# A fused decoder layer on one core: c spread by TensorE transposes, squares on two engines, sums of squares mixed with warm-up passes

## The chip, the core and the metric

The kernel runs on one core of a Trainium2 chip. The time is device microseconds of one execution. Engines are named as the profile names them: PE is TensorE's matmul side, PEld its weight loads, DVE VectorE, ACT ScalarE, POOL GpSimd, SP SyncE, which issues nearly all transfers (DMA) here.

## What is computed

One layer of a hybrid decoder over 256 positions of width 1024, in float32. A vector `c` conditions it:

```python
mod = jax.nn.silu(c) @ w_ada + b_ada            # 6 x 1024: shift, scale, gate, twice
h = rms_norm(x, norm1_g) * (1 + scale1) + shift1
x = x + gate1 * hybrid_token_mixer(h, ...)      # h @ w_in, attention and a state-space part, @ w_out
h = rms_norm(x, norm2_g) * (1 + scale2) + shift2
x = x + gate2 * conv_ffn(h, ...)                # up, causal conv, SwiGLU, down
```

What matters here is the start: `silu(c)`, the products of it with the rows of `w_ada`, and the mean square of every position of `x`, whose inverse root scales `h` ahead of the first projection.

## The kernel before

`x` stands transposed: `xT` has 128 partitions, 8 blocks `kt` of the width, 256 positions. All weights stream from HBM through a ring of eight raw buffers of 128x1024. Most are split into a high part (`whi`, ScalarE, L189) and a low part (`wlo`, VectorE, L191), and a product is three matmuls (high with high, low with high, high with low). The rows of `w_ada` come through buffers of their own (`ada`, `adax`); VectorE multiplies each with `silu(c)` and sums along the row (`ada_dve`, L239), which gives one column of `mod`.

`advance()` issues transfers on SyncE in a fixed list, and goes on as buffers come free. The first are `c`, two halves of `xT`, the first `ada`, part of `vec`, the second `ada`, then weights. `c` is read as one row into all 128 partitions of `cb` (L215), and ScalarE takes its silu in place (L233); `sc` is that tile.

From L221 to the end of the first stage every engine keeps the written order (`manual_schedule`); behind it a scheduler places the work of the stage that follows, on every engine. The front on TensorE:

- 22 passes of a matrix of ones with itself into bank 2 (L228), whose result nobody reads. They are the warm-up.
- `rms_sum` (L264): for each of the eight squared blocks two matmuls with one column of ones (L267), which add up the sums of squares for the two halves of the positions in bank 7. ScalarE takes the root (L270), VectorE the two `ada` products of `modulate1` and the reciprocal (L272).
- `keep_warm(n, out)` (L294) gives `n` more such passes: one here (`P["w0"]`), then `rms_transpose` (L289), two transposes that spread the result over the partitions, then four (`P["w1"]`).
- The first stage proper: for `kt` 0 matmuls with `hhi`, `hlo` (L412), the first v matmuls (`v0_mm`, L398), then the other blocks.

The squares `sq8` come from VectorE for blocks 0 to 3 (L325) and from ScalarE for 4 to 7 (L323), which loads the table for the root ahead of them (the activation into `warm`, L235). For `kt` 0, `s1_h` on ScalarE splits the first half of a weight chunk, writes `hhi`, `h` and `rb`, and then splits the second half; the first four matmuls use the first half, the next four the second. `v0_evac` copies the v results out of PSUM, half of them on ScalarE (L403), ahead of the next weight split there.

Of the kernel before, what the change touches and what calls it, by code (L numbers as in the profile page):

```python
# [11 lines left out]
AF = mybir.ActivationFunctionType  # L12
# [29 lines left out]
V_DTB = 326  # L42
V_ALL = 327

P = {'n2l': 6, 'sqa': 0, 'xr0': 0, 'scp': 1, 'vq': 1, 'v1': 6, 'n2': 4, 'hpx': [1, 0, 1, 0, 0, 1], 'e0': 0, 'ev': [1, 0, 1, 0], 'ada_u': [3, 4, 5, 5, 6, 7, 10, 9, 9, 19, 20, 20, 22, 24, 24, 25, 33, 35, 36, 37, 39, 39, 41, 42], 'ada_e': [1, 1, 1, 1, 1, 1, 1, 1, 1, 1, 1, 1, 1, 1, 1, 0, 1, 1, 1, 0, 1, 1, 0, 1], 'ada_lead': 4, 'ada_s': 0, 'g2': 68, 'hip': [0, 0, 0, 0, 0, 0, 0, 0, 0, 0, 0, 0, 0, 0, 0, 0, 0, 0, 0, 0, 0, 0, 0, 0, 0, 0, 0, 0, 0, 0, 1, 0, 0, 0, 1, 0, 0, 0, 0, 1, 0, 0, 0, 0, 0, 0, 0, 0, 0, 0, 0, 0, 0, 0, 0, 0, 0, 0, 0, 0], 'conv': [0, 0, 1, 0, 2, 5, 5, 4, 8, 4, 7, 6], 'dt': [1, 2, 2, 4], 'cdb': [7, 7], 'xbt': [9, 12, 11, 12], 'Y0': 14, 'DL': 3, 'ab0': 11, 'ss': 9, 'so': 2, 'qk': [12, 14, 17, 20, 21, 23], 'A0': 21, 'so1': 2, 'so2': 3, 'pv0': 26, 'sm_e': [0, 0, 1, 0, 1, 2, 2, 2], 'dc_e': [2, 0, 2, 0, 2, 0, 2, 0, 2, 0, 2, 0, 2, 0, 2, 0], 'mm_e': [1, 1, 1, 1, 1, 1, 1, 1, 1, 1, 1, 1, 1, 1, 1, 1], 'gz_e': [0, 0, 0, 0, 0, 0, 0, 0], 'sq_e': [1, 1, 1, 1, 1, 1, 1, 1], 'final': 2, 'ab_q': 0, 'LA': 2, 'asu': 34, 'aru': 38, 'aod': 2, 'w0': 1, 'w1': 4, 'w2': 4, 's1la': -1, 'zi': 1, 'lop': [0, 0, 0, 0, 0, 0, 0, 0, 0, 0, 0, 0, 0, 0, 0, 0, 0, 0, 0, 0, 0, 0, 0, 0, 0, 0, 0, 0, 0, 0, 0, 0, 0, 0, 0, 0, 0, 0, 0, 0, 0, 0, 0, 0, 0, 0, 0, 0, 0, 0, 0, 0, 0, 0, 0, 0, 0, 0, 0, 0], 'subs': [2, 1, 1, 1, 1, 1, 1, 1, 1, 1, 1, 1, 1, 1, 1, 1], 's1a': [0, 1, 0, 1, 0, 0, 0, 0]}

@with_exitstack
def mixer_ffn(ctx: ExitStack, tc: tile.TileContext, xT_d, c_d, vec_d, alog_d, ada_d,
# [155 lines left out]
    def get(la=LA):  # L204
        prep(la)
        i = st["get"]
        st["get"] += 1
        return ready.pop(i)

    cb = T([128, 1024], "cb")  # L210
    vec = T([128, V_ALL], "vec")
    alog = T([128, SH], "alog")
    xT = T([128, KT, S], "xT")

    sp.dma_start(cb, bass.AP(tensor=c_d.tensor, offset=c_d.offset, ap=[[0, 128], [1, D]]))  # L215
# [8 lines left out]
    pool.memset(epsc, EPS)  # L224
    ones = T([128, 128], "ones")
    pool.memset(ones, 1.0)
    for j in range(22):
        pe.matmul(bank[2][:, 0:128], ones, ones, start=True, stop=True)  # L228
    ident = T([128, 128], "ident")
    make_identity(nc, ident)  # L230
    mod = T([128, 48], "mod")
    sc = cb
    act.activation(sc, cb, AF.Silu)  # L233
    warm = T([128, 1], "warm")
    act.activation(warm, epsc, AF.Sqrt)  # L235

# [24 lines left out]
    rb2 = T([128, S], "rb2")  # L261
    acc = T([128, S], "accs")

    def rms_sum(parts, n, pb, between=lambda: None):  # L264
        for i, p in enumerate(parts):
            for t in range(2):
                pe.matmul(pb[:, t:t + 1], p[:, t * 128:(t + 1) * 128], ones[:, 0:1], start=(i == t == 0),  # L267
                          stop=(i == len(parts) - 1), skip_group_check=True)
        r = rt()
        act.activation(r[:, 2:4], pb[:, 0:2], AF.Sqrt, bias=epsc, scale=1.0 / n)  # L270
        between()
        dve.reciprocal(r[:, 0:2], r[:, 2:4])  # L272
        return r
# [15 lines left out]
    def rms_transpose(r, pb):  # L289
        for t in range(2):  # L290
            i = pe.transpose(pb[:, 256 + t * 128:384 + t * 128], r[:, t:t + 1].to_broadcast([128, 128]), ident)
        return i

    def keep_warm(n, out):  # L294
        for _ in range(n):
            pe.matmul(out, ones, ones, start=True, stop=True)
# [10 lines left out]
        return s  # L307


    sq8 = T([128, KT, S], "sq8", tag="big_x")  # L310
    sc1 = T([128, 2 * KT], "sc1")
    tri = T([128, 384], "tri")
    pool.memset(tri, 1.0)
# [43 lines left out]
    def s1_acc(i):  # L357
# [6 lines left out]
    final = (list(range(8)) + [12, 14, 15, 13, 8, 9, 10, 11], list(range(6)) + [14, 15, 12, 13, 8, 9, 10, 11, 6, 7],  # L364
             list(range(8)) + [14, 15, 12, 13, 8, 9, 10, 11], list(range(4)) + [14, 15, 12, 13, 8, 9, 10, 11, 4, 5, 6, 7])[P['final']]
# [58 lines left out]
    for kt in range(KT):  # L424
        if kt == 0:
# [5 lines left out]
            w0 = get(0)  # L431
# [310 lines left out]
    Y0, DL = P["Y0"], P["DL"]  # L742
# [21 lines left out]
    A0 = P["A0"]  # L764
# [23 lines left out]
    for i in range(5):  # L788
# [6 lines left out]
        c = st["get"] - 1  # L795
# [252 lines left out]
```

## Time and profile before

| | |
|---|---|
| three runs | 437.31, 437.0, 436.76 us; median 437.0 |
| the profiled execution | 437.12 us, of which the span is 435.4 us |
| PE / PEld / DVE / ACT / POOL busy | 98% / 89% / 78% / 59% / 8% of the span |
| chain that ended last | PE 84%, DVE 7%, ACT 5% |
| mean granted TensorE clock | 0.996 |
| HBM read | 95.14 MB, 221 GB/s over the span |

The span goes from the first to the last instruction; the time of a run has about 1.7 us around it. A row of the timeline gives the start, the length from the first start to the last end, engine, line, operation, what is written and read, the shape, how many, and in brackets the idle time ahead of it and what ended it. A matmul's recorded length is longer than its distance to the next one, since matmuls are pipelined: what a stream costs is read from the distance of starts. A float32 matmul of ones stands as two records (44 for 22 calls), a transpose as one.

### The profile page before, as it was taken

Reading aid. Unit: us, or ns where it says so; the run is one execution under the profiler, and the core shown is the slowest. Engines: PE = TensorE matmul, PEld = TensorE weight load, DVE = VectorE, ACT = ScalarE, POOL = GpSimd, SP = SyncE. Lnnn points to the kernel's source line nnn. Section 1 sums busy time; section 2 is a strip of 40 time slices with the busy share of each in tenths; the row PEclk is TensorE's granted clock in tenths of the full one; section 3 lists DMA queues with packets and bytes.
Section 4 is the critical chain, followed back from the end, with each engine's and each line's share of the span. In section 5 each row is a group of like instructions: output and inputs, shape, how many; then the busy total and the mean of one; then the engine's idle time right before and its main releaser. Section 6 shows DMA issues by size and latency. Waiting matters only on the chain.

```text
span 435.4 us, 7753 instructions
## 1 busy us (share of the span) xinstructions
PE 428.0 (98%) x2952; PEld 387.7 (89%) x2952; DVE 338.7 (78%) x670; ACT 259.0 (59%) x513; POOL 34.6 (8%) x31
## 2 busy tenths in 40 slices
PE   8999999999999999999999899999999999999996
PEld 9799998768766668888999699999999999999996
DVE  2779968999788998668699489787877876776655
ACT  4365448826998965642258386567766655555540
POOL 2000000000000020201220000032233200000000
PEclk9899999999999999999999999999999999999999
DMA  7999964899277644057790527866776565454002
GB/s 283 400 415 408 394 200 172 306 325 336 74 279 276 219 164 176 17 201 250 294 390 11 230 109 240 296 239 202 278 255 233 204 219 184 169 193 147 2 2 96
DMA packets 29589, 96.71 MB, mean 222 GB/s; under 512 B 3552, under 2 KB 6000, under 8 KB 29552
## 3 DMA queue, kind: packets, MB, share of 16 engines
q1 hardware_dynamic: 29520, 96.20, 61.1%
q8 instruction: 23, 0.38, 0.4%
q14 instruction: 14, 0.11, 0.1%
q10 hardware_dynamic: 32, 0.02, 0.0%
HBM read 95.14 MB, written 1.06 MB: 221 GB/s over the span
## 4 chain that ended last, share of the span: by engine, by line
PE 84%; DVE 7%; ACT 5%; issue 1%; DMA 1%; POOL 1%; ACTq 0%; POOLq 0%
PE bank L338 15%; PE bank L339 15%; PE bank L340 15%; PE bank L847 6%; PE bank L798 4%; PE bank L819 4%; PE bank L821 4%; PE bank L823 3%; PE bank L822 3%; DVE adax L239 2%; PE bank L412 2%; PE bank L228 2%; ACT whi L189 2%; DVE wlo L191 2%; PE bank L919 1%
## 5 line engine op out<-in xcount | busy, mean ns | idle before, releaser
L191 DVE TENSOR_TENSOR wlo<-raw,whi 128x1024 fp32r<-128x1024 f32 (+2 forms) x107 | 132.8, 1242 | 17.8 <-ACT whi L189 17.7
L189 ACT ACTIVATE whi<-raw 128x1024 fp32r<-128x1024 f32 (+2 forms) x106 | 108.6, 1032 | 39.8 <-PE bank L340 23.7
L338 PE MATMUL bank<-h2hi,whi 128*128 128x256 f32 x336 | 95.4, 285 | 2.1 <-ACT h2hi L889 1.9
L339 PE MATMUL bank<-h2hi,wlo 128*128 128x256 f32 x336 | 94.5, 283 | 0.0
L340 PE MATMUL bank<-h2lo,whi 128*128 128x256 f32 x336 | 93.9, 284 | 0.0
L338 PEld LDWEIGHTS bank<-h2hi,whi 128*128 128x128 f32 x336 | 64.4, 192 | 3.7 <-ACT h2hi L889 3.2
L339 PEld LDWEIGHTS bank<-h2hi,wlo 128*128 128x128 f32 x336 | 64.4, 192 | 0.0
L340 PEld LDWEIGHTS bank<-h2lo,whi 128*128 128x128 f32 x336 | 63.8, 192 | 0.2 <-DVE h2lo L890 0.2
L905 DVE SCALAR_TENSOR_TENSOR fbuf<-bank,vec,fbuf 128x255 f32<-128x255 f32 x84 | 40.3, 481 | 29.4 <-ACT fbuf L903 28.1
L244 POOL TENSOR_TENSOR ada<-ada,cb 128x1024 f32<-128x1024 f32 x11 | 28.8, 2621 | 270.2 <-DMA ada<-in_ada_dram 270.2
L338 PE MATMUL bank<-fsp,whi 128*128 128x256 f32 x176 | 49.8, 284 | 0.0
L339 PE MATMUL bank<-fsp,wlo 128*128 128x256 f32 x176 | 49.7, 283 | 0.0
L340 PE MATMUL bank<-fsp,whi 128*128 128x256 f32 x176 | 49.6, 283 | 0.0
L903 ACT ACTIVATE fbuf<-bank,vec 128x256 f32<-128x256 f32 x42 | 23.4, 560 | 36.2 <-PE bank L340 36.2
L239 DVE SCALAR_TENSOR_TENSOR ada<-ada,cb 128x1024 f32<-128x1024 f32 x27 | 32.8, 1216 | 3.0 <-DMA ada<-in_ada_dram 3.0
L338 PEld LDWEIGHTS bank<-fsp,whi 128*128 128x128 f32 x176 | 33.8, 192 | 0.1
L339 PEld LDWEIGHTS bank<-fsp,wlo 128*128 128x128 f32 x176 | 33.8, 192 | 0.0
L340 PEld LDWEIGHTS bank<-fsp,whi 128*128 128x128 f32 x176 | 33.7, 192 | 0.0
L821 PE MATMUL bank<-whi,hhi 128*128 128x512 f32 x70 | 29.5, 422 | 0.0
L847 PE MATMUL bank<-y,raw 128*128 128x256 f32 x128 | 28.9, 380 | 0.0
L822 PE MATMUL bank<-wlo,hhi 128*128 128x512 f32 x70 | 28.6, 408 | 0.0
L823 PE MATMUL bank<-whi,hlo 128*128 128x512 f32 x70 | 28.3, 405 | 0.0
(214 smaller groups left out, 783.1 us busy)
## 6 DMA issues: line engine op xcount, KB each, us to landing
raw<-in_wup_dram SPq DMA_DIRECT2D x44, 512.0 KB, 4.1
ada<-in_ada_dram SPq DMA_DIRECT2D x38, 512.0 KB, 5.1
raw<-in_wdn_dram SPq DMA_DIRECT2D x22, 512.0 KB, 3.6
raw<-in_winq_dram SPq DMA_DIRECT2D x16, 512.0 KB, 4.8
raw<-in_wout_dram SPq DMA_DIRECT2D x16, 512.0 KB, 3.8
adax<-in_ada_dram SPq DMA_DIRECT2D x10, 512.0 KB, 9.6
raw<-in_win_dram SPq DMA_DIRECT2D x8, 456.0 KB, 9.7
raw<-in_win_dram SPq DMA_DIRECT2D x7, 512.0 KB, 9.8
```

The source lines that it names most:

```text
L189: act.activation(hi[:, c], t[:, c], AF.Copy)
L191: (pool if lo_on_pool(i) else dve).tensor_tensor(lo[:, c], t[:, c], hi[:, c].bitcast(F32), op=OP.subtract)
L239: dve.scalar_tensor_tensor(t, t, 1.0, sc, op0=OP.mult, op1=OP.mult, accum_out=mod[:, i:i + 1])
L244: pool.tensor_tensor(adas[i], adas[i], sc, op=OP.mult)
L338: pe.matmul(out, w[0], h[0], start=start, stop=False, skip_group_check=True)
L339: pe.matmul(out, w[1], h[0], start=False, stop=False, skip_group_check=True)
L340: pe.matmul(out, w[0], h[1], start=False, stop=stop, skip_group_check=True)
L821: pe.matmul(bs[t], hhi[:, kt, blk(t)], w[0][:, wc], start=(q4 == k2 == 0), stop=False)
L822: pe.matmul(bs[t], hhi[:, kt, blk(t)], w[1][:, wc], start=False, stop=False)
L823: pe.matmul(bs[t], hlo[:, kt, blk(t)], w[0][:, wc], start=False, stop=(kt == KT - 1))
L847: pe.matmul(sacc(d), w[:, blk(kt)], X["y32"][:, kt], start=(kt == d % 2 == 0), stop=(kt == 7), skip_group_check=True)
L905: dve.scalar_tensor_tensor(a[:, s:], src[:, :S - s], vec[:, w + 2 - s:w + 3 - s], a[:, s:], op0=OP.mult, op1=OP.add)
```

## The change

- `c` comes as a tile `ccol` of 128 partitions by 8 columns (the host lays it out so). Eight TensorE transposes, each of one column broadcast to 128 wide, write it to banks 0 and 1, so that every partition has all of c; ScalarE takes the silu of each bank into one half of `cb`.
- The first warm-up has 10 passes instead of 22; eight passes stand behind the c transposes.
- ScalarE squares blocks 4 and 5 ahead of the table load, VectorE 0, 1, 2, 3, 6 and 7.
- `rms_sum` gets `fill`: ahead of every pair of sum matmuls but the first, three passes. The blocks are summed in the order 0, 1, 2, 3, 4, 6, 5, 7.
- Five passes stand ahead of the root's transposes instead of one, eight behind them instead of four. `P["w0"]` becomes 4 and is read by nobody.

```diff
-    sp.dma_start(cb, bass.AP(tensor=c_d.tensor, offset=c_d.offset, ap=[[0, 128], [1, D]]))
+    ccol = T([128, KT], "ccol")
+    sp.dma_start(ccol, c_d)
...
-    for j in range(22):
+    for j in range(10):
         pe.matmul(bank[2][:, 0:128], ones, ones, start=True, stop=True)
     ident = T([128, 128], "ident")
     make_identity(nc, ident)
+    for j in range(KT):
+        pe.transpose(bank[j // 4][:, j % 4 * 128:j % 4 * 128 + 128], ccol[:, j:j + 1].to_broadcast([128, 128]), ident)
     mod = T([128, 48], "mod")
     sc = cb
-    act.activation(sc, cb, AF.Silu)
+    act.activation(sc[:, 0:512], bank[0], AF.Silu)
+    sq8 = T([128, KT, S], "sq8", tag="big_x")
+    act.activation(sc[:, 512:1024], bank[1], AF.Silu)
+    for kt in (4, 5):
+        act.activation(sq8[:, kt], xT[:, kt], AF.Square)
...
-    def rms_sum(parts, n, pb, between=lambda: None):
+    def rms_sum(parts, n, pb, between=lambda: None, fill=None):
         for i, p in enumerate(parts):
+            if fill and i:
+                keep_warm(fill, bank[2][:, 0:128])
             for t in range(2):
...
-    for kt in range(4, KT):
-        act.activation(sq8[:, kt], xT[:, kt], AF.Square)
-    for kt in range(4):
+    for kt in (0, 1, 2, 3, 6, 7):
         dve.tensor_tensor(sq8[:, kt], xT[:, kt], xT[:, kt], op=OP.mult)
...
-    r1 = rms_sum([sq8[:, kt] for kt in range(KT)], D, bank[7], modulate1)
-    keep_warm(P["w0"], bank[2][:, 0:128])
+    keep_warm(8, bank[2][:, 0:128])
+    r1 = rms_sum([sq8[:, kt] for kt in (0, 1, 2, 3, 4, 6, 5, 7)], D, bank[7], modulate1, 3)
+    keep_warm(5, bank[2][:, 0:128])
     rms_transpose(r1, bank[7])
-    keep_warm(P["w1"], bank[2][:, 0:128])
+    keep_warm(8, bank[2][:, 0:128])
...
-    arr["c"] = a["c"]
+    arr["c"] = cols(a["c"][0])
```

TensorE's list at the front, before (bank_67 is bank 2, bank_72 bank 7, `rt` the root; a count stands behind x):

```order
L228 MATMUL bank_67<-ones 128x128 x22
L267 MATMUL bank_72<-ones,sq_180 128x1 x16
L296 MATMUL bank_67<-ones 128x128
L291 MATMUL bank_72<-ident,rt_172 128x128 x2
L296 MATMUL bank_67<-ones 128x128 x4
L412 MATMUL bank_65<-hhi,whi_81 128x256 x2
```

The start of the same list in the changed kernel (line numbers are seven or more higher there; L276 are the sums, L305 the passes):

```order
L229 MATMUL bank_67<-ones 128x128 x10
L233 MATMUL bank_65<-ident,ccol 128x128 x4
L233 MATMUL bank_66<-ident,ccol 128x128 x4
L305 MATMUL bank_67<-ones 128x128 x8
L276 MATMUL bank_72<-ones,sq_158 128x1 x2
L305 MATMUL bank_67<-ones 128x128 x3
```

The last two rows alternate until the eighth pair of sums. The end of the front, changed kernel:

```order
L276 MATMUL bank_72<-ones,sq_158 128x1 x2
L305 MATMUL bank_67<-ones 128x128 x5
L300 MATMUL bank_72<-ident,rt_173 128x128 x2
L305 MATMUL bank_67<-ones 128x128 x8
L419 MATMUL bank_65<-hhi,whi_81 128x256 x2
```

Between the first pass and the first matmul of the stage stand 43 matmuls and 2 transposes before, and 68 matmuls (16 of them sums in either), 8 transposes of c and 2 of the root in the changed kernel.

ScalarE's list at its start, before:

```order
L233 ACT_TABLE_LOAD
L233 ACTIVATE cb<-cb 128x1024
L235 ACT_TABLE_LOAD
L235 ACTIVATE warm<-epsc 128x1
L323 ACTIVATE sq_180<-xT 128x256 x4
L270 ACTIVATE rt_172<-bank_72,epsc 128x2
```

And in the changed kernel:

```order
L236 ACT_TABLE_LOAD
L236 ACTIVATE cb<-bank_65 128x512
L238 ACTIVATE cb<-bank_66 128x512
L240 ACTIVATE sq_158<-xT 128x256 x2
L242 ACT_TABLE_LOAD
L242 ACTIVATE warm<-epsc 128x1
L279 ACTIVATE rt_173<-bank_72,epsc 128x2
```

The silu now reads what TensorE wrote instead of a transfer, and two of the squares stand ahead of the second table load.

Behind the first stage the scheduler's order differs too. VectorE where the convolutions (`cv`, L506) begin, before:

```order
L506 SCALAR_TENSOR_TENSOR cv_759<-bank_70,vec,cv_759 128x253
L506 SCALAR_TENSOR_TENSOR cv_758<-bank_69,vec,cv_758 128x255
L506 SCALAR_TENSOR_TENSOR cv_757<-bank_65,vec,cv_757 128x255
L506 SCALAR_TENSOR_TENSOR cv_758<-bank_69,vec,cv_758 128x254
L506 SCALAR_TENSOR_TENSOR cv_760<-bank_70,vec,cv_760 128x255
```

The same place in the changed kernel:

```order
L513 SCALAR_TENSOR_TENSOR cv_794<-bank_70,vec,cv_794 128x253
L191 TENSOR_TENSOR wlo_87<-raw_73,whi_82 128x1024
L513 SCALAR_TENSOR_TENSOR cv_793<-bank_69,vec,cv_793 128x255
L246 SCALAR_TENSOR_TENSOR ada_91,mod<-ada_91,cb 128x1024
L513 SCALAR_TENSOR_TENSOR cv_793<-bank_69,vec,cv_793 128x254
```

A weight split and an `ada` product have moved ahead of convolution steps there. From the first stage's first matmul to its end the order of every engine is unchanged.

## Rows read from the trace of the kernel before

**Rows 1.** The page: its head, and the engine line (busy us, share, instructions).

```profile
span 435.4 us, 7753 instructions
PE 428.0 (98%) x2952; PEld 387.7 (89%) x2952; DVE 338.7 (78%) x670; ACT 259.0 (59%) x513; POOL 34.6 (8%) x31
```

**Rows 2.** The chain of waits, 0 to 45 us: start, us, what.

```profile
1.09 7.55 PE bank L228 x44
...
18.62 3.45 PE bank L398 x8
...
22.09 0.60 ACT vS L403
22.69 0.94 ACT whi L189
```

**Rows 3.** Timeline of PE, 5.9 to 18.6 us, several stretches (the second within the first).

```profile
5.52 3.12 PE L228 MATMUL bank<-ones 128*128 128x128 f32 x24
...
6.46 2.17 PE L228 MATMUL bank<-ones 128*128 128x128 f32 x18
...
8.47 3.63 PE L267 MATMUL bank<-ones,sq 128*128 128x1 f32 x32
...
11.96 0.47 PE L296 MATMUL bank<-ones 128*128 128x128 f32 x2
...
12.75 0.51 PE L291 MATMUL bank<-ident,rt 128*128 128x128 f32 x2 [0.32 <-DVE gcol L373]
...
13.05 1.92 PE L296 MATMUL bank<-ones 128*128 128x128 f32 x8
...
14.62 2.08 PE L412 MATMUL bank<-hhi,whi 128*128 128x256 f32 x8
...
18.46 3.60 PE L398 MATMUL bank<-raw,h 128*128 128x512 f32 x8
```

**Rows 4.** Busy time by stretches: length, engines' busy us (records), PEclk, DMA share, GB/s.

```profile
0.00:6.00 6.00, 4.91 (x23) 4.91 (x24) 0.00 (x0) 2.23 (x2) 2.21 (x13) 1.00 0.55 215
12.50:13.00 0.50, 0.25 (x2) 0.28 (x3) 0.29 (x3) 0.42 (x1) 0.00 (x0) 0.92 1.06 426
13.00:16.00 3.00, 3.00 (x15) 2.85 (x14) 1.79 (x4) 1.97 (x5) 0.00 (x0) 0.50 1.03 420
16.00:16.50 0.50, 0.50 (x4) 0.50 (x4) 0.50 (x2) 0.50 (x1) 0.00 (x0) 0.67 1.13 442
24.00:60.00 36.00, 36.00 (x298) 35.15 (x296) 33.44 (x63) 19.02 (x28) 0.00 (x0) 1.00 0.95 373
64.00:180.00 116.00, 115.80 (x567) 86.05 (x566) 101.43 (x274) 87.33 (x241) 3.17 (x3) 1.00 0.62 222
241.00:251.00 10.00, 8.11 (x47) 6.38 (x45) 5.77 (x15) 3.86 (x8) 0.00 (x0) 1.00 0.72 278
260.00:430.00 170.00, 170.00 (x1419) 170.00 (x1419) 130.12 (x186) 100.70 (x153) 19.91 (x8) 1.00 0.54 185
```

**Rows 5.** Timeline of DVE and ACT, 0 to 16 us.

```profile
6.31 1.43 DVE L325 TENSOR_TENSOR sq<-xT 128x256 f32<-128x256 f32 x4 [6.31 <-DMA xT<-in_xT_dram]
...
7.75 1.33 ACT L323 ACTIVATE sq<-xT 128x256 f32<-128x256 f32 x4
...
9.25 1.23 DVE L239 SCALAR_TENSOR_TENSOR ada<-ada,cb 128x1024 f32<-128x1024 f32 x1 [1.51 <-DMA ada<-in_ada_dram]
...
13.75 0.60 ACT L385 ACTIVATE hhi<-hbuf,mod,gcol 128x256 fp32r<-128x256 f32 x1 [0.83 <-DVE hbuf L378]
...
15.01 0.62 ACT L189 ACTIVATE whi<-raw 128x512 fp32r<-128x512 f32 x1
```

**Rows 6.** Transfers of the whole run: what, queue, count, KB each, us to landing.

```profile
out_dram<-obuf SPq DMA_DIRECT2D x3, 256.0 KB, 2.0
cb<-in_c_dram SPq DMA_DIRECT2D x1, 512.0 KB, 4.2
...
acd<-acT ACTq DMA_DIRECT2D x1, 16.0 KB, 5.8
```

More of the change, by code (lines that the diff above doesn't have):

```diff
@@ L43 @@
 V_ALL = 327
-P = {'n2l': 6, 'sqa': 0, 'xr0': 0, 'scp': 1, 'vq': 1, 'v1': 6, 'n2': 4, 'hpx': [1, 0, 1, 0, 0, 1], 'e0': 0, 'ev': [1, 0, 1, 0], 'ada_u': [3, 4, 5, 5, 6, 7, 10, 9, 9, 19, 20, 20, 22, 24, 24, 25, 33, 35, 36, 37, 39, 39, 41, 42], 'ada_e': [1, 1, 1, 1, 1, 1, 1, 1, 1, 1, 1, 1, 1, 1, 1, 0, 1, 1, 1, 0, 1, 1, 0, 1], 'ada_lead': 4, 'ada_s': 0, 'g2': 68, 'hip': [0, 0, 0, 0, 0, 0, 0, 0, 0, 0, 0, 0, 0, 0, 0, 0, 0, 0, 0, 0, 0, 0, 0, 0, 0, 0, 0, 0, 0, 0, 1, 0, 0, 0, 1, 0, 0, 0, 0, 1, 0, 0, 0, 0, 0, 0, 0, 0, 0, 0, 0, 0, 0, 0, 0, 0, 0, 0, 0, 0], 'conv': [0, 0, 1, 0, 2, 5, 5, 4, 8, 4, 7, 6], 'dt': [1, 2, 2, 4], 'cdb': [7, 7], 'xbt': [9, 12, 11, 12], 'Y0': 14, 'DL': 3, 'ab0': 11, 'ss': 9, 'so': 2, 'qk': [12, 14, 17, 20, 21, 23], 'A0': 21, 'so1': 2, 'so2': 3, 'pv0': 26, 'sm_e': [0, 0, 1, 0, 1, 2, 2, 2], 'dc_e': [2, 0, 2, 0, 2, 0, 2, 0, 2, 0, 2, 0, 2, 0, 2, 0], 'mm_e': [1, 1, 1, 1, 1, 1, 1, 1, 1, 1, 1, 1, 1, 1, 1, 1], 'gz_e': [0, 0, 0, 0, 0, 0, 0, 0], 'sq_e': [1, 1, 1, 1, 1, 1, 1, 1], 'final': 2, 'ab_q': 0, 'LA': 2, 'asu': 34, 'aru': 38, 'aod': 2, 'w0': 1, 'w1': 4, 'w2': 4, 's1la': -1, 'zi': 1, 'lop': [0, 0, 0, 0, 0, 0, 0, 0, 0, 0, 0, 0, 0, 0, 0, 0, 0, 0, 0, 0, 0, 0, 0, 0, 0, 0, 0, 0, 0, 0, 0, 0, 0, 0, 0, 0, 0, 0, 0, 0, 0, 0, 0, 0, 0, 0, 0, 0, 0, 0, 0, 0, 0, 0, 0, 0, 0, 0, 0, 0], 'subs': [2, 1, 1, 1, 1, 1, 1, 1, 1, 1, 1, 1, 1, 1, 1, 1], 's1a': [0, 1, 0, 1, 0, 0, 0, 0]}
@@ new lines @@
+P = {'n2l': 6, 'sqa': 0, 'xr0': 0, 'scp': 1, 'vq': 1, 'v1': 6, 'n2': 4, 'hpx': [1, 0, 1, 0, 0, 1], 'e0': 0, 'ev': [1, 0, 1, 0], 'ada_u': [3, 4, 5, 5, 6, 7, 10, 9, 9, 19, 20, 20, 22, 24, 24, 25, 33, 35, 36, 37, 39, 39, 41, 42], 'ada_e': [1, 1, 1, 1, 1, 1, 1, 1, 1, 1, 1, 1, 1, 1, 1, 0, 1, 1, 1, 0, 1, 1, 0, 1], 'ada_lead': 4, 'ada_s': 0, 'g2': 68, 'hip': [0, 0, 0, 0, 0, 0, 0, 0, 0, 0, 0, 0, 0, 0, 0, 0, 0, 0, 0, 0, 0, 0, 0, 0, 0, 0, 0, 0, 0, 0, 1, 0, 0, 0, 1, 0, 0, 0, 0, 1, 0, 0, 0, 0, 0, 0, 0, 0, 0, 0, 0, 0, 0, 0, 0, 0, 0, 0, 0, 0], 'conv': [0, 0, 1, 0, 2, 5, 5, 4, 8, 4, 7, 6], 'dt': [1, 2, 2, 4], 'cdb': [7, 7], 'xbt': [9, 12, 11, 12], 'Y0': 14, 'DL': 3, 'ab0': 11, 'ss': 9, 'so': 2, 'qk': [12, 14, 17, 20, 21, 23], 'A0': 21, 'so1': 2, 'so2': 3, 'pv0': 26, 'sm_e': [0, 0, 1, 0, 1, 2, 2, 2], 'dc_e': [2, 0, 2, 0, 2, 0, 2, 0, 2, 0, 2, 0, 2, 0, 2, 0], 'mm_e': [1, 1, 1, 1, 1, 1, 1, 1, 1, 1, 1, 1, 1, 1, 1, 1], 'gz_e': [0, 0, 0, 0, 0, 0, 0, 0], 'sq_e': [1, 1, 1, 1, 1, 1, 1, 1], 'final': 2, 'ab_q': 0, 'LA': 2, 'asu': 34, 'aru': 38, 'aod': 2, 'w0': 4, 'w1': 4, 'w2': 4, 's1la': -1, 'zi': 1, 'lop': [0, 0, 0, 0, 0, 0, 0, 0, 0, 0, 0, 0, 0, 0, 0, 0, 0, 0, 0, 0, 0, 0, 0, 0, 0, 0, 0, 0, 0, 0, 0, 0, 0, 0, 0, 0, 0, 0, 0, 0, 0, 0, 0, 0, 0, 0, 0, 0, 0, 0, 0, 0, 0, 0, 0, 0, 0, 0, 0, 0], 'subs': [2, 1, 1, 1, 1, 1, 1, 1, 1, 1, 1, 1, 1, 1, 1, 1], 's1a': [0, 1, 0, 1, 0, 0, 0, 0]}
@@ L307, in square_add @@
         return s
-    sq8 = T([128, KT, S], "sq8", tag="big_x")
     sc1 = T([128, 2 * KT], "sc1")
```

## The prediction

> **What bounds the kernel now.** I read the page's engine line first, then the chain of waits over the first 45 us, then the TensorE timeline of the same stretch, and last the busy time by stretches, to learn whether a shift at the front reaches the end.
>
> The page gives TensorE 98% of the span [rows 1]. Busy time can hide stalls, so I count. From 24 to 60 us there are 298 matmul records in 36.00 us, 0.121 us each; from 260 to 430 us 1419 records in 170.00 us, 0.120 each; between 64 and 180 us 0.2 us of 116 stand idle [rows 4]. One record (a "pass record" below) costs what its stream costs, and TensorE streams nearly without a gap. The one stretch with gaps, 241 to 251 us (8.11 busy of 10), waits for the second norm, which hangs on TensorE's own earlier work and which the change leaves alone. So **a delay of TensorE's work at the front is carried to the end**: nothing behind it has slack to absorb it.
>
> At the front, the chain runs 1.09 to 8.6 us over the 22 warm-up passes (L228), then over the sums of squares (L267), the root, its two transposes and L412 to the v matmuls L398, which end at 22.07; from there it goes through ScalarE's copy and its next weight split (L189) [rows 2]. The squares are not what it waits for: VectorE's four are done at 7.74, ScalarE's four at 9.08 [rows 5], while TensorE, in order, reaches the first sum at 8.47 and needs 3.49 us for 32 records [rows 3]. TensorE's own list sets the front.
>
> Its pace there: the last 24 records of the 44 begin at 5.52, so the first 20 took (5.52 - 1.09) / 20 = 0.22 us each; from 6.46 to 8.47 eighteen take 0.112 each [rows 3]. From 13.05 eight records again take 0.21 each, at a granted clock of 0.50 (1.2 GHz), while the row 0 to 6 us prints 1.00 [rows 3, 4]. I trust the pace: half clock up to about 6 us, 2.4 GHz from there, and half again from 12.9 (0.92 in the row from 12.5) to 16.3 (0.67 in the row from 16.0) [rows 4].
>
> **The change part by part.** A float32 128x128 matmul is two records (44 for 22 calls), a transpose one (2 for 2 calls).
>
> *The first 44 records.* Before: 44 records of passes, first sum at 8.47. After: 10 passes are 20 records and end where record 21 begins now, at 5.52; then 8 transposes and 8 passes, 8 + 16 = 24 records in the place of the 24 that now fill 5.52 to 8.47. A transpose stands in no row at a settled clock; its bounds are a pass record at full and at half clock, 0.112 and 0.21 us. I take the lower, since the clock rises at 6 us in either kernel: **0**, up to +0.8. The transposes also need the 4 KB of c. The small transfers of this trace land 2.0 to 5.8 us after issue, c's 512 KB took 4.2 [rows 6]; issued at 0.80 it is there at 2.8 to 6.6, wanted at 5.52. I take no wait, since first in an empty queue it is nearest to the 2.0 and 4.2; the far end is +1.1.
>
> *Silu in two halves and the squares.* ScalarE's silu waits for the transposes, until some 7 us; then two halves, two squares, the table load. VectorE has six squares at 0.36 and then the two ada products. All of it is wanted only when the sums end; now the last ScalarE square is done at 9.08 and the first ada product runs from 9.25 [rows 5]. The cover is TensorE's longer list (next item), 4 us of it; if it were gone, the later silu would cost about 1 us. **0.**
>
> *Sums with three passes between the pairs.* The 32 sum records stay at 3.49 us. Seven times three passes are 42 records more, at 0.112 us: **+4.69**. They stand in TensorE's queue ahead of the remaining sums, and nothing makes TensorE wait there now (32 records in 3.49 us is 0.109 each, without a gap), so they fill no hole. Sums end at 11.96 + 4.69 = 16.65.
>
> *Five passes instead of one ahead of the root's transposes.* Now 0.79 us go by from the last sum (11.96) to the transposes (12.75), for ScalarE's root and VectorE's reciprocal [rows 3]. Ten records are 1.12 us, so the passes last longest: **+0.33**, transposes at 17.77.
>
> *Eight passes instead of four behind them.* Now 1.87 us from the transposes to the first L412 (14.62) [rows 3]. Two transposes and 16 records at full clock are 2.01; h's first half is written 1.60 after the transposes (13.75 + 0.60 - 12.75) [rows 5], so passes last again: **+0.14**, first L412 at 19.78.
>
> *The clock of the first matmuls.* From the first L412 to the first v matmul now 14.62 to 18.46, 3.84 us for 24 records, the first part at half clock. At 0.121 they are 2.90. But four in, TensorE needs the second half of the split weights, which ScalarE has ready 2.88 us after the transposes (15.01 + 0.62 - 12.75) [rows 5], at 20.65: 0.39 after the four are through. So 3.3: **-0.50**; bounds -0.94 (no wait) and 0.
>
> *c's transfer.* 512 KB at 420 GB/s [rows 4] are 1.25 us of transfers that all later ones gain. No wait for a transfer stands on the chain behind 1.09 us, so **0**; SP's queue passes nothing.
>
> *The order behind the first stage.* The scheduler places the work from 64 us on anew: a weight split and an ada product move ahead of convolution steps on VectorE. What hides it is TensorE's own queue of plain matmuls there, which idles 0.2 us from 64 to 180. A gain cannot exceed that idle time; for a loss the nearest row is the 1.89 us that TensorE idles where it does wait for VectorE and ScalarE (241 to 251) [rows 4]. I take **0**, nearer to the gap-free rows.
>
> **Sum:** 4.69 + 0.33 + 0.14 - 0.50 = +4.66 us; bounds from 4.69 + 0.33 + 0.14 - 0.94 - 0.2 = +4.0 to 5.16 + 0.8 + 1.1 + 1.9 = +9.0 with all bad ends at once. The profiled execution took 437.12 (span 435.4, 1.7 around it), the median of the three runs is 437.0: 437.0 + 4.6 = **441.6**.
>
> **The rivals.**
> *A: the clock falls although passes are mixed in.* Now it fell at 12.9, after 3.5 us of one-column sums and 0.45 us of idling. In the new kernel 4 of every 10 records are still such sums. Against it: at 241 to 251 us TensorE is idle almost a fifth of the time and the granted clock stays 1.00 [rows 4]. One low stretch here is about 3.4 us long (12.9 to 16.3) and costs half of that: +1.7, **443.3**.
> *B: the transposes hold the clock down.* If the eight transposes at 5.52 do not count as work, the rise at 6 us comes one stretch later, and 3.4 us go at half pace: +1.7, also **443.3**. They are 0.5 of the 5 us ahead of the rise, so I hold it for unlikely. The Trainium skill, "TensorE: Matmul & The Clock Gate", section "Part 4: PE-mode transpose", says that transposes do not count as TensorE being busy for its clock; no row here shows it, and by that rule the time would be this rival's.
> *C, on the other side: transfers pace the front.* VectorE waits 6.31 us for x and 1.51 for ada [rows 5]. If first x and then the weights come last, the 25 extra TensorE passes fill waiting time, and what counts is the 1.25 us less of c: 437.0 - 1.25 - 0.5 = **435.3**. It decides if squares or weights are ready later than the passes ahead of them end, near 16 us; they are there by 9.08 and 15.0, in a kernel with the longer c transfer. Little speaks for it.
> *D: the new order stalls TensorE once* between 64 and 180 us, as long as the norm's wait: +1.9, **443.5**.
>
> **How the numbers follow.** Forecast 0.74; A 0.09; B 0.05; D 0.06; C 0.06. The likeliest time is 441.6. The range takes in A, B and D at the top, and some way below the sum's lower bound (441.0) at the bottom, since a gain that no row shows can come with the new order: 439.8 to 443.9; C and a combination of bad ends are left out. Below 0.2% (0.9 us, about what a measurement of this kernel can tell from no change) only C ends faster (0.05 of its 0.06; 0.01 within); a large gain from the new order could bring it to no change (0.02): faster 0.05, same 0.03, slower 0.92.
>
> **What would show it.** Right: the first sum near 8.5 us, the last near 16.6, sums and passes without gaps at 0.11 us a record, the root's transposes near 17.8, v matmuls from 23, everything behind it 4 to 5 us later, no half-clock row after 6 us. Wrong: a gap ahead of the c transposes or between sums (something other than TensorE's list sets the front); a stage from 24 to 60 us that is shorter than now (transfers or VectorE paced it, C); a row with clock 0.50 near 9 to 13 us (A) or 6 to 9 us (B); TensorE gaps between 64 and 180 us (D).

## The result, and the profile after

| | us | ratio to the kernel before | n |
|---|---|---|---|
| before, on the same chip | 437.14 (436.76 to 437.31) | | 4 |
| changed | 441.56 (441.32 to 441.94) | 1.0108, 95% interval 1.0096 to 1.012 | 4 |

The change costs 4.4 us; 441.6 was forecast. The profiled execution of the changed kernel took 441.94 us, 4.82 more than the profiled one of before (437.12). Line numbers are about seven higher: L229 are the first passes, L233 the transposes of `c`, L276 the sums, L305 all other passes, L300 the root's transposes, L419 the first matmuls, L405 the v matmuls.

The page's head and engine line, changed kernel (compare [rows 1]):

```profile
span 440.2 us, 7877 instructions
PE 431.9 (98%) x3010; PEld 391.3 (89%) x3010; DVE 341.6 (78%) x672; ACT 258.3 (59%) x512; POOL 33.5 (8%) x31
```

The span is 4.8 us longer, and TensorE is busy 3.9 us longer: its share stays 98%, as one expects where work was added to the engine that sets the time. The chain of waits, changed kernel, 0 to 18 us (start, us, what; compare [rows 2]):

```profile
1.09 3.95 PE bank L229 x20
5.04 0.87 PE bank L233 x8
5.92 1.79 PE bank L305 x16
7.70 0.34 PE bank L276 x4
8.04 0.78 PE bank L305 x6
...
15.86 1.22 PE bank L305 x10
17.08 0.23 PE bank L300 x2
```

From 1.09 to 17.3 us every link is TensorE's: no transfer, no silu, no square stands in it. Its timeline (start, us; compare [rows 3]):

```profile
4.88 1.04 PE L233 MATMUL bank<-ident,ccol 128*128 128x128 f32 x8
5.75 1.95 PE L305 MATMUL bank<-ones 128*128 128x128 f32 x16
7.54 0.50 PE L276 MATMUL bank<-ones,sq 128*128 128x1 f32 x4
7.91 0.92 PE L305 MATMUL bank<-ones 128*128 128x128 f32 x6
...
15.36 0.50 PE L276 MATMUL bank<-ones,sq 128*128 128x1 f32 x4
15.72 1.36 PE L305 MATMUL bank<-ones 128*128 128x128 f32 x10
16.92 0.38 PE L300 MATMUL bank<-ident,rt 128*128 128x128 f32 x2
17.14 1.95 PE L305 MATMUL bank<-ones 128*128 128x128 f32 x16
18.84 0.71 PE L419 MATMUL bank<-hhi,whi 128*128 128x256 f32 x4
19.73 0.74 PE L419 MATMUL bank<-hhi,whi 128*128 128x256 f32 x4 [0.17 <-ACT whi L189]
...
22.20 3.60 PE L405 MATMUL bank<-raw,h 128*128 128x512 f32 x8
```

No row from 4.88 to 18.84 carries idle time. The eight transposes take 0.87 us, 0.11 each (4.88 to 5.75). Sums with their passes run from 7.54 to 15.72: 8.18 us for 74 records, 0.11 each. The v matmuls begin at 22.20, against 18.46.

Four more rows say how much of the rest hung on this list: the root on ScalarE, the transfer of `c` (columns as [rows 6], where the old one took 4.2 us), and busy time in two stretches (columns as [rows 4]).

```profile
15.90 0.26 ACT L279 ACTIVATE rt<-bank,epsc 128x2 f32<-128x2 f32 x1 [6.54 <-PE bank L276]
```

```profile
ccol<-in_c_dram SPq DMA_DIRECT2D x1, 4.0 KB, 1.7
```

```profile
13.00:16.00 3.00, 3.00 (x29) 3.00 (x28) 0.00 (x0) 0.10 (x1) 0.00 (x0) 1.00 1.02 405
64.00:180.00 116.00, 114.99 (x569) 85.73 (x569) 99.96 (x269) 85.25 (x234) 2.44 (x1) 1.00 0.63 227
```

ScalarE stood idle 6.54 us ahead of the root, waiting for the sums. `c` was there 1.7 us after its issue. The granted clock is 1.00 where before had 0.50. And TensorE idles 1.0 us between 64 and 180 us, where before idled 0.2; experiments 9 to 11 say how much of that is the new order's.

### The profile page after: what moved, and what is told of

Its sections match the earlier page's. It is cut to its first block, busy times and chain, and to the rows that moved or that the text cites. A ratio compares the mean times of both kernels' runs of the same rounds, so it can differ in the third digit from the quotient of the medians.

```text
span 440.2 us, 7877 instructions
## 1 busy us (share of the span) xinstructions
PE 431.9 (98%) x3010; PEld 391.3 (89%) x3010; DVE 341.6 (78%) x672; ACT 258.3 (59%) x512; POOL 33.5 (8%) x31
## 4 chain that ended last, share of the span: by engine, by line
PE 76%; DVE 9%; DMA 7%; ACT 5%; issue 2%; POOL 1%; SPq 0%; ACTq 0%; POOLq 0%
PE bank L345 13%; PE bank L346 13%; PE bank L347 13%; PE bank L854 6%; DMA ada<-in_ada_dram 4%; PE bank L805 4%; PE bank L828 4%; PE bank L830 4%; PE bank L829 3%; PE bank L826 3%; DVE wlo L191 3%; PE bank L305 2%; DMA raw<-in_win_dram 2%; ACT whi L189 1%; PE bank L419 1%
## 5 line engine op out<-in xcount | busy, mean ns | idle before, releaser
L191 DVE TENSOR_TENSOR wlo<-raw,whi 128x1024 fp32r<-128x1024 f32 (+2 forms) x107 | 137.5, 1286 | 17.1 <-ACT whi L189 17.0
L347 PEld LDWEIGHTS bank<-h2lo,whi 128*128 128x128 f32 x336 | 63.8, 192 | 0.2 <-DVE h2lo L897 0.2
L251 POOL TENSOR_TENSOR ada<-ada,cb 128x1024 f32<-128x1024 f32 x11 | 27.8, 2524 | 275.2 <-DMA ada<-in_ada_dram 275.2
L854 PE MATMUL bank<-y,raw 128*128 128x256 f32 x128 | 28.9, 380 | 0.0
```

What stands on the lines that cost most here:

```text
L191: (pool if lo_on_pool(i) else dve).tensor_tensor(lo[:, c], t[:, c], hi[:, c].bitcast(F32), op=OP.subtract)
L251: pool.tensor_tensor(adas[i], adas[i], sc, op=OP.mult)
L347: pe.matmul(out, w[0], h[1], start=False, stop=stop, skip_group_check=True)
L854: pe.matmul(sacc(d), w[:, blk(kt)], X["y32"][:, kt], start=(kt == d % 2 == 0), stop=(kt == 7), skip_group_check=True)
```

## The experiments

Each kernel differs from the one named by the lines shown. The table gives where TensorE stands in each profiled execution (us, from start to start: first v matmul, the time from there to the first out-projection matmul L854, and from there to the last matmul of L926, the plain up projection of the FFN) and the medians. Line numbers are the changed kernel's. From that last L926 to the start of the last matmul of all, every kernel needs 189.0 us, to 0.03. Behind the first stage, kernels 1 to 8 and 11 have the kernel before's order of work, 9 and 10 the changed kernel's. That holds for VectorE and ScalarE, and by the traces for TensorE too: some 70 records of its own list, the first at 72 us, stand elsewhere in the new order.

| kernel | first sum | first root transpose | first v | v to L854 | L854 to last L926 | median (n), before on its chip |
|---|---|---|---|---|---|---|
| before | 8.47 | 12.75 | 18.46 | 160.6 | 63.6 | 437.14 (4) |
| changed | 7.54 | 16.92 | 22.20 | 161.1 | 64.2 | 441.56 (4), 437.14 |
| 1 no passes between sums | 8.61 | 13.37 | 19.78 | 160.6 | 63.4 | 437.60 (10), 436.99 |
| 2 before + passes | 8.12 | 17.09 | 22.42 | 160.8 | 63.3 | 441.05 (4), 436.99 |
| 3 before + columns of c | 7.56 | 11.76 | 17.34 | 160.3 | 63.4 | 436.72 (10), 436.99 |
| 4 one pass between | 7.84 | 16.33 | 22.22 | 160.5 | 63.4 | 440.57 (4), 436.99 |
| 5 four passes ahead of root | 7.64 | 16.80 | 22.09 | 160.6 | 63.2 | 440.55 (6), 436.98 |
| 6 passes in holes only | 6.45 | 11.70 | 17.25 | 160.5 | 63.4 | 437.22 (12), 436.98 |
| 7 as 6, wide sums | 6.42 | 11.44 | 16.72 | 160.6 | 63.2 | 435.58 (12), 436.98 |
| 8 before, wide sums | 7.92 | 12.30 | 17.63 | 160.8 | 63.6 | 436.81 (12), 436.98 |
| 9 seven passes behind root | 8.76 | 18.14 | 23.43 | 161.5 | 63.9 | 442.57 (5), 437.27 |
| 10 changed, again | 7.92 | 17.30 | 22.59 | 161.1 | 63.8 | 441.92 (4), 437.27 |
| 11 as 5, again | 7.48 | 16.64 | 21.95 | 160.6 | 63.6 | 440.60 (5), 437.27 |

**1. The passes between the pairs, taken out of the changed kernel.**

```diff
-    r1 = rms_sum([sq8[:, kt] for kt in (0, 1, 2, 3, 4, 6, 5, 7)], D, bank[7], modulate1, 3)
+    r1 = rms_sum([sq8[:, kt] for kt in (0, 1, 2, 3, 4, 6, 5, 7)], D, bank[7], modulate1)
```

> The changed kernel without the three passes between the pairs of sums; all else stays. Theory 1 (TensorE's own list sets the front, so every pass ahead of the root's transposes costs its 0.112 us a record): 42 records less, 4.7 us, 441.6 - 4.7 = 436.9 us, if the clock stays up; last sum near 11.0 in the trace instead of 15.7. Theory 2 (the passes also hold the clock): the clock falls to half soon after the sums, as it did in the kernel before at 12.9; then the eight passes behind the transposes cost 16 x 0.1 us more and the first matmuls half a us, about 438.7 to 439. Rival (the passes fill waiting time for squares or transfers): the time stays above 440.

Measured 437.60 us (437.26 to 438.27), 1.0014 of before, interval 1.0005 to 1.0024. Timeline of PE and one stretch (columns as [rows 4]):

```profile
8.61 3.63 PE L276 MATMUL bank<-ones,sq 128*128 128x1 f32 x32
12.10 1.47 PE L305 MATMUL bank<-ones 128*128 128x128 f32 x10
13.37 0.64 PE L300 MATMUL bank<-ident,rt 128*128 128x128 f32 x2
13.79 3.31 PE L305 MATMUL bank<-ones 128*128 128x128 f32 x16
16.86 1.19 PE L419 MATMUL bank<-hhi,whi 128*128 128x256 f32 x8
```

```profile
13.50:16.50 3.00, 3.00 (x16) 3.00 (x15) 1.54 (x4) 2.01 (x5) 0.00 (x0) 0.50 1.05 416
```

The clock falls again: the sixteen records from 13.79 need 3.07 us, 0.19 each, where the changed kernel needs 1.70, and root transpose to first v takes 6.41 us instead of 5.28. So the passes do hold the clock, and what they hold is worth about 1.1 us in this profile, at a price of 4.69. It does not fall in every execution: in two of the ten the mean granted clock is 1.00, and these took 437.26 and 437.32 us, 0.3 less than the median of the other eight. The median lies between the two branches written down; 4.0 us below the changed kernel, some of which is the order (experiments 5 and 9 to 11).

**2. The passes alone, put into the kernel before.**

```diff
-    r1 = rms_sum([sq8[:, kt] for kt in range(KT)], D, bank[7], modulate1)
+    r1 = rms_sum([sq8[:, kt] for kt in range(KT)], D, bank[7], modulate1, 3)
```

with the lines of the change that give `rms_sum` its `fill`.

> The kernel before with three passes between the pairs of sums, nothing else of the change. Theory 1: +4.7 us for 42 records, less about 0.3 for four passes that now run at full clock and 0.5 for the first matmuls, so 437.1 + 3.9 = 441.0 us, within 0.6 of the changed kernel; no half-clock row after the first 6 us. If the passes did not hold the clock: 437.1 + 4.7 = 441.8 or more, with a row of 0.50 near 12 to 17 us. Rival (it is the c transposes and the later silu that cost): 437 to 438.

Measured 441.05 us (440.73 to 441.70), 1.0093 of before, interval 1.0078 to 1.0108: as expected. PE's timeline and one stretch:

```profile
8.12 0.50 PE L269 MATMUL bank<-ones,sq 128*128 128x1 f32 x4
...
17.09 0.40 PE L293 MATMUL bank<-ident,rt 128*128 128x128 f32 x2 [0.32 <-DVE gcol L375]
```

```profile
17.00:20.00 3.00, 2.12 (x15) 1.75 (x15) 1.67 (x6) 2.27 (x6) 0.00 (x0) 1.00 1.04 394
```

First sum to first root transpose grows from 4.28 to 8.97 us, +4.69 for 42 records, 0.112 each, and the granted clock stays at 1.00. Nearly the whole cost of the change comes with this line.

**3. The columns of `c` alone, in the kernel before.** `ccol`, ten first passes, the eight transposes, eight passes, silu in two halves; sums, squares and their order stay.

```diff
-    sp.dma_start(cb, bass.AP(tensor=c_d.tensor, offset=c_d.offset, ap=[[0, 128], [1, D]]))
+    ccol = T([128, KT], "ccol")
+    sp.dma_start(ccol, c_d)
...
+    for j in range(KT):
+        pe.transpose(bank[j // 4][:, j % 4 * 128:j % 4 * 128 + 128], ccol[:, j:j + 1].to_broadcast([128, 128]), ident)
+    for j in range(8):
+        pe.matmul(bank[2][:, 0:128], ones, ones, start=True, stop=True)
```

> The kernel before with c as 8 columns alone: 10 passes, 8 transposes, 8 passes ahead of the sums and the silu in two halves; squares, sums and later passes as before. Theory 1: 24 records in the place of 24, and the later silu is hidden: 437.1 us, within 0.4. If the transposes keep the clock down: half-clock pace past 6 us, +1.7, 438.8. If transfers paced the front: 1.25 us less, 435.9.

Measured 436.72 us (435.41 to 439.58), 0.9997 of before, interval 0.9976 to 1.0019: no difference that can be measured, as expected. By the interval, the half megabyte less to read and the transposes together move the time by no more than -1.0 to +0.8 us. Nor do the transposes hold the clock down here: in the profile the passes ahead of them already run at full pace, and they do too.

```profile
4.90 1.04 PE L233 MATMUL bank<-ident,ccol 128*128 128x128 f32 x8
5.78 1.95 PE L235 MATMUL bank<-ones 128*128 128x128 f32 x16
7.56 3.64 PE L273 MATMUL bank<-ones,sq 128*128 128x1 f32 x32
```

**4. One pass between the pairs instead of three.**

```diff
-    r1 = rms_sum([sq8[:, kt] for kt in (0, 1, 2, 3, 4, 6, 5, 7)], D, bank[7], modulate1, 3)
+    r1 = rms_sum([sq8[:, kt] for kt in (0, 1, 2, 3, 4, 6, 5, 7)], D, bank[7], modulate1, 1)
```

> The changed kernel with one pass between the pairs of sums instead of three. Theory 1: 28 records less at 0.112, 441.6 - 3.1 = 438.5 us, if one pass between pairs is enough to hold the clock; if the clock falls as in the kernel before, 1.6 to 2 us more, about 440.3. Rival (passes fill waiting time): above 441.

Measured 440.57 us (440.22 to 441.09), 1.0081 of before, interval 1.0063 to 1.0098: the second branch. Two stretches (columns as [rows 4]):

```profile
8.00:11.50 3.50, 3.50 (x35) 3.50 (x33) 2.60 (x6) 1.48 (x2) 0.00 (x0) 1.00 1.04 396
12.00:18.00 6.00, 6.00 (x30) 6.00 (x29) 1.35 (x5) 1.32 (x4) 0.00 (x0) 0.50 1.03 405
```

TensorE is busy without a gap in both, 10 records per us in the first and 5 in the second: with two streaming records for every four one-column sums the clock fell all the same, for twice as long as in the kernel before ([rows 4]: 0.50 from 13 to 16). This is rival A's mechanism. It did not reach the changed kernel, where six streaming records stand to four sums.

**5. Four passes instead of five ahead of the root's transposes.** With this the scheduler gives back, on every engine, the order that the kernel before has behind the first stage.

```diff
-    keep_warm(5, bank[2][:, 0:128])
+    keep_warm(4, bank[2][:, 0:128])
     rms_transpose(r1, bank[7])
```

> The changed kernel with four passes instead of five ahead of the root's transposes. On the engines behind the first stage this gives back the order of the kernel before (the scheduler's order changes with the fifth pass). Theory 1: the front gets one pass shorter, 0.22 us, and the work behind the first stage loses the 1 us that its profile shows against the kernel before: 440.2 to 440.6, with 63.5 us instead of 64.2 from the first out projection to the last matmul of the plain up projection. Rival (the order costs nothing, the changed kernel's profile was only a slow execution): 441.3.

Measured 440.55 us (440.27 to 441.77), 1.008 of before, interval 1.0057 to 1.0103: one microsecond below the changed kernel, of which the pass itself accounts for 0.2 (first sum to first v takes 14.45 us instead of 14.66).

**6. Passes only where TensorE would wait.** Eight passes ahead of the sums and those between them are left out; six stand ahead of the root's transposes, four behind.

```diff
-    keep_warm(8, bank[2][:, 0:128])
-    r1 = rms_sum([sq8[:, kt] for kt in (0, 1, 2, 3, 4, 6, 5, 7)], D, bank[7], modulate1, 3)
-    keep_warm(5, bank[2][:, 0:128])
+    r1 = rms_sum([sq8[:, kt] for kt in (0, 1, 2, 3, 4, 6, 5, 7)], D, bank[7], modulate1, None)
+    keep_warm(6, bank[2][:, 0:128])
     rms_transpose(r1, bank[7])
-    keep_warm(8, bank[2][:, 0:128])
+    keep_warm(4, bank[2][:, 0:128])
```

> The changed kernel with passes only where TensorE would wait: ten, the c transposes, the sums at once and without passes between, six passes ahead of the root's transposes, four behind. Theory 1: the sums end near 9.7 us, VectorE's two ada products (to 11.1) then set the transposes, near 11.4, and the first matmul, near 13.0 instead of 18.8 (14.6 before). At full clock the v matmuls would start near 16.3, 2.1 us ahead of the kernel before: 435.0; if the clock falls after the sums as it did before, 1 to 1.7 more: 436.0 to 436.7. Rival (squares or transfers are late when nothing covers them): no faster than the kernel before, 437 or more.

Measured 437.22 us (435.63 to 438.54), 1.0004 of before, interval 0.9988 to 1.0019: a miss. PE's timeline and one stretch of the profiled execution:

```profile
6.45 3.73 PE L276 MATMUL bank<-ones,sq 128*128 128x1 f32 x32 [0.44 <-DVE sq L331]
```

```profile
11.50:14.50 3.00, 3.00 (x16) 3.00 (x15) 1.46 (x4) 1.67 (x4) 0.00 (x0) 0.50 1.03 410
```

This execution, the fastest, has one low stretch like that of before and a mean clock of 0.996; ten of the twelve have 0.992, which is twice the time at half clock. A shorter head brings the sums forward until they wait 0.44 us for a square, and the clock pays back the gain. The second part is read from the mean clocks; none of the ten was profiled.

**7. The same, with sums that stream.** Each sum matmul multiplies with all 128 columns of ones instead of one; of the result one column is read.

```diff
-                pe.matmul(pb[:, t:t + 1], p[:, t * 128:(t + 1) * 128], ones[:, 0:1], start=(i == t == 0),
+                pe.matmul(pb[:, t * w:t * w + w], p[:, t * 128:(t + 1) * 128], ones[:, 0:w], start=(i == t == 0),
...
-        act.activation(r[:, 2:4], pb[:, 0:2], AF.Sqrt, bias=epsc, scale=1.0 / n)
+        act.activation(r[:, 2:4], pb[:, 0:2 * w:w], AF.Sqrt, bias=epsc, scale=1.0 / n)
```

with `w=128` in the first call of `rms_sum`, and the passes of experiment 6.

> As the run with passes only where TensorE would wait, but each sum matmul streams all 128 columns of ones instead of one (the root reads one column of each). A sum matmul costs 0.22 us already for its weight load, so the columns should be free and do the work of the passes between. Theory 1: clock stays up, 434.8 to 435.3. If 128 columns cost more than the load: sums end later, 0.11 us per record more, 3.5 us at most, 438.

Measured 435.58 us (434.84 to 436.03), 0.9959 of before, interval 0.9945 to 0.9972. It beats both kernels. PE's timeline, then a stretch of the same length and place as [rows 4] show at half clock:

```profile
6.42 3.84 PE L276 MATMUL bank<-ones,sq 128*128 128x128 f32 x32
10.10 1.50 PE L305 MATMUL bank<-ones 128*128 128x128 f32 x12
...
12.97 0.74 PE L418 MATMUL bank<-hhi,whi 128*128 128x256 f32 x4 [0.25 <-ACT hhi L391]
14.25 0.73 PE L418 MATMUL bank<-hhi,whi 128*128 128x256 f32 x4 [0.54 <-ACT whi L189]
...
16.72 3.60 PE L404 MATMUL bank<-raw,h 128*128 128x512 f32 x8
```

```profile
11.50:14.50 3.00, 2.21 (x17) 1.82 (x16) 1.72 (x4) 1.88 (x4) 0.00 (x0) 1.00 1.03 409
```

The 32 records take 3.68 us (6.42 to 10.10), against 3.49 with one column in the kernel before [rows 3] and 3.59 in experiment 6: streaming 128 columns instead of one costs 0.1 to 0.2 us in all, and the clock stays at 1.00 behind them although TensorE idles a quarter of that stretch. The front is now bound by ScalarE, which is late with `hhi` and `whi`.

**8. Sums that stream, in the kernel before.** The two lines of experiment 7 alone.

> The kernel before with the sum matmuls streaming 128 columns of ones instead of one; nothing else. Measures what the clock at the front is worth by itself. Theory 1: no half-clock row after 6 us; four passes at full clock 0.3 and the first matmuls 0.5 us shorter, 436.2 to 436.5, last sum at 11.9 as now. If the fall of the clock had another cause than the single columns: 437.0 and a row of 0.50 near 13 to 16.

Measured 436.81 us (436.22 to 439.83), 0.9997 of before, interval 0.9979 to 1.0014: no difference that can be measured, where 436.2 to 436.5 was expected. One stretch:

```profile
13.00:16.00 3.00, 2.20 (x17) 1.81 (x16) 2.08 (x5) 1.88 (x4) 0.00 (x0) 1.00 1.05 423
```

In the profile the clock holds and v begins 0.83 us earlier, 0.55 of it because the first sum does (7.92 against 8.47). Root transpose to first v is 5.33 us, 0.38 less than before. A held clock alone is worth no more than that here.

**9 to 11. Order or pass?** Experiment 5 took away a pass and changed the order at once. Here the changed kernel runs beside two kernels with one pass less: one keeps the changed kernel's order on every engine (seven passes instead of eight behind the root's transposes), one has the order of before (experiment 5 again).

```diff
-    keep_warm(8, bank[2][:, 0:128])
+    keep_warm(7, bank[2][:, 0:128])
 
     def mm3(out, w, h, start, stop):
```

> The changed kernel with seven passes instead of eight behind the root's transposes: one pass less, while every engine behind the first stage keeps the changed kernel's order. Theory (the order is what the run with four passes ahead of the transposes gave back, some 0.8 to 1 us, and a pass is worth its list price of 0.11 to 0.22 us): 0.1 to 0.3 us below the changed kernel, so 441.3 to 441.4 where that has 441.56, with a stall of TensorE near 164 us as in the changed kernel. Rival (what that run gave back came from the pass at the front, or from chance): about 1 us below the changed kernel, 440.6.

> The changed kernel itself, on the same chip as its two neighbours. Both theories: 441.3 to 441.8.

> The changed kernel with four passes instead of five ahead of the root's transposes, once more, on the same chip as the changed kernel: one pass less, and the kernel before's order behind the first stage. Theory: 440.4 to 440.7, 0.9 to 1.2 us below the changed kernel and 0.7 to 0.9 below the kernel with seven passes behind. Rival: as the kernel with seven passes behind the transposes, within 0.3 us.

Measured: 442.57 us (441.58 to 443.25; 1.0113, interval 1.0096 to 1.013), 441.92 (441.75 to 442.42; 1.0108, 1.0094 to 1.0122) and 440.60 (440.48 to 441.46; 1.0079, 1.0066 to 1.0093). Where a pass went and the order stayed, nothing was gained; where the order went back, 1.3 us, of which 0.2 is the pass. The rival falls. My number for the first was 1.2 us too low: in its profiled execution, the slowest of the five, the first sum comes late, at 8.76, and TensorE waits once more than in the changed kernel, here ahead of other transposes. Its timeline:

```profile
20.95 0.74 PE L419 MATMUL bank<-hhi,whi 128*128 128x256 f32 x4 [0.40 <-ACT whi L189]
...
117.84 0.66 PE L668 MATMUL bank<-ident,qk 128*128 128x128 f32 x4 [0.47 <-DVE xdt L569]
...
166.47 0.33 PE L668 MATMUL bank<-ident,qk 128*128 128x128 f32 x1 [0.83 <-ACT qk L662]
```

The first row also prices the eighth pass: with seven, TensorE waits 0.40 us for the second half of the split weights, with eight 0.17, and root transpose to first v takes 5.29 and 5.28 us. It was free.

The wait for `qk` in the changed kernel, and where it comes from (PE, ACT):

```profile
163.54 0.48 PE L828 MATMUL bank<-whi,hhi 128*128 128x512 f32 x1
164.39 1.86 ACT L662 ACTIVATE qk<-qk,rqk 128x128 f32<-128x128 f32 x6 [1.58 <-DVE rqk L296]
164.84 0.33 PE L668 MATMUL bank<-ident,qk 128*128 128x128 f32 x1 [0.82 <-ACT qk L662]
```

TensorE waits 0.82 us for ScalarE, which waited 1.58 us for VectorE's `rqk`. The kernel before has no such row, but the wait is not the new order's alone. Kernels 1, 2, 4, 5 and 11, with the old order and a first v at 19.78 or later, have it with 0.54 to 0.57 us; in kernel 11:

```profile
164.27 0.33 PE L668 MATMUL bank<-ident,qk 128*128 128x128 f32 x1 [0.57 <-ACT qk L662]
```

From first v to L854 these five need 160.5 to 160.8 us, the kernel before 160.6. Between 64 and 180 us TensorE idles 0.6 to 0.8 us in them. The new order's share of the wait is thus about 0.3: the row stands 142.64 us behind the first v in the changed kernel, 142.32 in kernel 11. In both, the same `ada` products and weight splits stand ahead of that `rqk` on VectorE; the new order has one `gcol` (0.2 us) more there.

Behind the first out-projection matmul there are two smaller waits in the changed kernel, 0.12 us (187.70) and, at the sums of the second norm, this one:

```profile
244.32 0.61 PE L276 MATMUL bank<-ones,sq 128*128 128x1 f32 x4 [0.28 <-ACT sq L313]
```

It is missing from the changed kernel's second profile, so that one is not the order's doing alone. These waits do not add up to the whole difference; the rest was not traced to a wait. The table gives the sum: from the first v to the last L926 the three profiles with the new order need 224.8 to 225.4 us, the ten with the old one 223.7 to 224.4; the means are 225.2 and 224.0.

## Why the prediction was right, and where it was not

The total was right, by its main step and by two misses that cancel.

| step | forecast | profiles |
|---|---|---|
| passes between the pairs | +4.69 | +4.69 (8.18 us from first to last sum and pass, for 3.49) |
| five passes ahead of the root's transposes | +0.33 | +0.41 (1.20 for 0.79) |
| eight behind | +0.14 | +0.05 (1.92 for 1.87) |
| clock of the first matmuls | -0.50 | -0.48 (3.36 for 3.84) |
| first 44 records | 0 | -0.93 (first sum at 7.54 for 8.47) |
| order behind the first stage | 0 | +1.10 (0.50 ahead of L854, 0.60 behind) |
| sum | +4.66 | +4.84; the two profiled executions differ by 4.82, the medians by 4.42 |

**The front went as worked out.** That TensorE's own list sets the front, and that an added record costs what its stream costs, is shown twice: by taking the 42 records out (experiment 1) and by putting them alone into the kernel before (2). Root transposes came at 16.92 for 17.77, v at 22.20 for "from 23"; both are earlier by the head alone.

**First 44 records, mis-sized by chance.** The order and count of records were right, and the transposes took the pace of a pass. But the clock rose at 4.2 us in the profiled execution, not at 6: the first sum behind the same 44 records stands at 7.48, 7.54, 7.56, 7.64, 7.84, 7.92, 8.61 and 8.76 us in eight profiles (kernels 11, changed, 3, 5, 4, 10, 1, 9), and at 7.92, 8.12 and 8.47 with the old head (8, 2, before). The two sets overlap, so I take most of the 0.93 for the execution's, not the change's; a few tenths these profiles can't settle. I had read one execution's 6 us as a constant.

**Three readings behind small terms were off.** By its own terms the clock's item is 3.29 for 3.84, so -0.55 and not -0.50. The idle time ahead of the fall was 0.32 us by the row, not 0.45 [rows 3]. And the 2.0 us taken for a small transfer belongs to 256 KB of output [rows 6]; the transfer of `c` took 1.7, so that it came in time owes something to luck.

**The order, wrongly set to 0.** The step that failed is the one that called TensorE's gap-free queue a cover. It covered less than that: the kernels with the new order need 1.2 us more from the first v to the last L926, by the means. The prediction also looked at VectorE's order alone, where TensorE's list moved as well. The bound (+1.9) held. Rival D, one stall between 64 and 180 us, came in part: that stall is some 0.3 us longer by the new order, 0.50 us of the 1.10 lie ahead of L854, and 0.60 behind it, where D placed none. That the order as a whole costs this is shown; which of its instructions, on which engine, costs which part was not separated.

**The other rivals.** A: the granted clock of the changed kernel is 1.00 from 13 to 16 us; its mechanism exists, and shows with one pass between the pairs (4). B and C, each priced at some 1.7 us: the columns of `c` alone move the time by -1.0 to +0.8 us at most (3). The Trainium skill, "TensorE: Matmul & The Clock Gate", section "Part 4: PE-mode transpose", gives about 275 ns for a transpose in a kernel and says that transposes do not count as busy for the clock. The eight here, queued back to back, cost 0.11 us each by the distance of starts; a single one is on record with a length of 0.33 us (L668 at 164.84). Whether they count stays open. In the changed kernel and in experiment 3 the engine was at full pace before and behind them. In experiments 1 and 9 it was still at half pace when they began; this is experiment 1:

```profile
5.52 1.47 PE L233 MATMUL bank<-ident,ccol 128*128 128x128 f32 x8
6.82 1.95 PE L305 MATMUL bank<-ones 128*128 128x128 f32 x16
```

The eight took 1.30 us there and 1.45 in experiment 9, so the clock rose while they ran. These are the two latest rises of the thirteen profiles, but the later of them, at some 6.7 us, is 0.7 behind the 6 us of the kernel before and not 3.4, as B has it.

## What to carry to other kernels

A warm-up pass in an in-order queue is free only where the engine would have waited; ahead of work that is ready it costs its whole stream, here 0.11 us a record, and a held clock was worth 0.4 to 1.1 us in the profiles, against 4.7. Where needed matmuls are too thin to keep the clock, widen them instead of adding idle ones: the same weights with 128 columns for one cost 0.1 to 0.2 us over 32 records and kept it (experiment 7). And an edit at the front that makes a scheduler place the rest anew is two changes; a neighbour of the edit with the old order tells them apart.

## What the runs showed of the hardware

- The clock's first rise moves from one execution to the next: by the pace of the records (0.22 us before it, 0.11 behind) it came between some 4.1 and 6.7 us in these profiles, which moves everything behind by up to 1.3 us (first sum 7.48 to 8.76). The Trainium skill, same page, section "What you observe", has it vary from run to run by 0.5 us either way; here it was over twice that.
- The row of granted clocks prints 1.00 from the start of the span, while the first passes take 0.22 us each; only the pace shows the first rise.
- With every record back to back and no idle time, the granted clock fell to 0.50 behind one-column sums (1, by the mean clock in eight of ten executions) and behind sums with one pass between (4); it stayed at 1.00 behind sums with three passes (2) and behind 128-column sums (7, 8).
- Executions of one kernel differ more than the interval of a median suggests: kernel 3 went from 435.41 to 439.58 us, kernel 8 took 439.83 once beside eleven of 436.2 to 437.2. Both of these slowest ones have a mean granted clock 0.004 below most executions of their kernel, but two executions of the kernel before with 0.990 instead of 0.996 took 437.2 and 437.35 us, so that is not all of it. None of them was profiled, and the cause stays open.
